# Recurrent merge tiles of a hybrid decoder layer: four of eight as two pairs by seven products

## The chip, the cores and the metric

The kernel runs on one core of one Trainium2 chip. The metric is the device time of one execution in microseconds. Before the change it is 872.28 us, the median of 3 runs (871.96 to 872.85).

## The reference

One inference step of one decoder layer over 512 prompt positions and 8 samples, so 520 columns; all in float32. The parts that the change touches:

```python
z = rmsnorm(x, g1) @ w_in                  # 1024 x 6656, column blocks for three mixers and three gates
h, h_last = rg_lru(conv(b_x), ...)         # recurrent branch
yb = gelu(b_gate) * h                      # b_gate: 1024 columns of z
ga, gb, gc = split(sigmoid(gates))         # 3 x 1024 columns of z
merged = ga * (ya @ w_pa) + gb * (yb @ w_pb) + gc * (yc @ w_pc)
x = x + merged @ w_o
h = gelu(causal_dwconv(xn2 @ wg)) * (xn2 @ wu)      # FFN, 3072 columns
x = x + h @ wd
```

## The kernel before

Everything lies feature by column: a tile of an activation is 128 features by 520 columns, and a weight tile is 1024 x 128, that is eight blocks of 128 x 128 (`Chunk`). A float32 product is made of three matmuls in fp32r: high part by high part, high by low, low by high. The high part is a copy on ScalarE (`high`, L117), the low part the difference to it on VectorE (`low`, L126). A plain tile is 8 blocks x 3 x 2 halves of 260 columns, 48 matmuls.

**Pairs by seven products.** Two output tiles can be made together (`Pair`): weights and input are each cut into 2 x 2 quarters, and seven products of 12 matmuls replace the eight of a plain computation, 84 matmuls where two plain tiles take 96. The products need sums of weight quarters (`sums`, two arrays h2 and h3, on VectorE, and their high and low parts, L189 and L192) and seven forms of the input (`X`), four of which (numbers 2, 3, 4, 6) are sums and differences, each with a high and a low part (`operand`). The results are put together from three PSUM banks and copies of what bank 0 and bank 2 held on the way (`run_pair`, the copies at L267). Input 0, 1 and 5 are halves of tiles that are there anyway. Before the change the four pairs of recurrent gates (`T_GB`) and the FFN tiles from the fifth on are made this way.

**Order.** Time is counted in tiles: `now` goes on by 1 for a plain tile, 0.125 for each of its eight blocks, and by 0.25 for each product of a pair. Each step of a weight tile or a pair has a time ahead of its start (`steps`, in quarters; `at`), and each step behind an output a time after it (`after`). Steps are put into the engines' queues in order of these times, and each queue is worked off in order. A pair goes through `SEQ_PAIR`, its products and, between them, the quarters of one more plain tile (the "filler", or two half-length tiles in the FFN); the first two FFN pairs, whose low parts are made by DMA (`by_dma`), go through `SEQ_FIRST`.

**The stretch that is changed.** Four plain tiles of the recurrent gate (`bg_parts`, times 44 to 48), each followed by `bg_post`: gelu on ScalarE, multiplication with h on VectorE (L843), high part on ScalarE (L433), low part on VectorE (L434). Then four gate pairs of 2.75 tiles each, with the other four `bg_parts` as fillers; their outputs (`gb_out`) go through a sigmoid and to DRAM (`gbd`). Their sums of the input are made from rows that `rows_in` (L884) reads back from DRAM (`xsd`), at times 42 and 43 (`XG`), a step every 0.6. Then eight plain merge tiles (`w_pb`, times 59 to 67), each with `pb_post`: multiplication with the gate (L880), addition of the other branches (L881), high and low part. `pb_load` brings the gate and the sum of the other branches two tiles ahead, and at the fifth tile `reload_x` reads all eight tiles of x at once for the output projection. Then eight `w_o` tiles, the second norm, and the FFN. Its first tiles are plain; the first pair comes behind them, and its fillers take the inputs hh[0] to hh[3], which `u2_post` and `later_hilo` (L1044) make from the last plain tiles.

The tiles of activations share 57 buffers of one size.

## Time and profile before

| | |
|---|---|
| median of 3 runs | 872.28 us |
| profiled execution, its own time | 872.23 us |
| its span | 870.5 us |
| mean granted TensorE clock | 0.993 |
| TensorE busy | 853.9 us, 7072 matmuls |
| VectorE busy | 620.3 us, 953 instructions |
| ScalarE busy | 476.9 us, 728 instructions |
| GpSimd busy | 159.2 us, 241 instructions |
| DMA | 124.89 MB, mean 143 GB/s |

The span is from the first to the last instruction of the profiled execution. The profile also divides it into stretches, lists what ended each engine's idle time (its releaser), and gives instructions in order of time. A matmul's end is modelled, so consecutive matmuls overlap in the list; what counts is the distance of their starts.

### The profile page before, as it was taken

The page shows a single profiled execution, that of the slowest core. Times are in us where ns is not written, and L with a number is a line of the kernel's source. Part 1 is how long each engine was busy: PE and PEld are TensorE (multiplying, and loading weights), DVE is VectorE, ACT ScalarE, POOL GpSimd, SP SyncE. Part 2 cuts the span into 40 slices and gives each one's busy share as a digit, 9 for nine tenths or more (in the row PEclk, how much of TensorE's full clock was granted, in tenths as well). Part 3 has the DMA queues.
Part 4 walks back from the last instruction along what each step waited for, and adds up shares of the span by engine and source line. Part 5 has one row for each costly group of instructions (what it writes and reads, how often), then busy time and mean ns, then how long its engine had stood idle before and what let it go on. Part 6 is the DMA issues. An engine that isn't in the chain of part 4 may idle for free.

```text
span 870.5 us, 17032 instructions
## 1 busy us (share of the span) xinstructions
PE 853.9 (98%) x7072; PEld 847.8 (97%) x7072; DVE 620.3 (71%) x953; ACT 476.9 (55%) x728; POOL 159.2 (18%) x241
## 2 busy tenths in 40 slices
PE   8999999999999999999999989999999999999996
PEld 7999999999999999999999989999999999999995
DVE  5797998698773876455553995776777777768655
ACT  7555464478341565542346785646656556556542
POOL 0522412111114000150012111011011110110143
PEclk9999999999999999999999999999999999999997
DMA  8464234322246633583349776555655555555642
GB/s 279 143 212 123 66 105 137 124 94 88 83 111 181 182 129 105 171 324 116 123 158 235 159 178 136 143 133 122 159 110 145 137 112 155 135 121 150 156 99 99
DMA packets 42254, 124.89 MB, mean 143 GB/s; under 512 B 5289, under 2 KB 8873, under 8 KB 42153
## 3 DMA queue, kind: packets, MB, share of 16 engines
q1 hardware_dynamic: 25872, 83.08, 30.6%
q0 software_dynamic: 14784, 39.17, 20.4%
q10 hardware_dynamic: 1520, 1.57, 0.5%
q8 instruction: 55, 0.90, 0.4%
q14 instruction: 23, 0.18, 0.1%
HBM read 100.09 MB, written 24.09 MB: 143 GB/s over the span
## 4 chain that ended last, share of the span: by engine, by line
PE 85%; DVE 8%; ACT 4%; issue 1%; DMA 1%; SPq 0%; POOL 0%; DVEq 0%; ACTq 0%; POOLq 0%
PE pj L211 57%; PE pa L263 15%; PE c L263 7%; PE pf L263 4%; PE lru L211 1%; DVE wl L192 1%; DVE b L993 1%; ACT wh L189 1%; DVE d L827 1%; DVE fc L971 1%; DVE bg L843 1%; DMA x<-in_x 1%; ACT yb_h L433 0%; ACT wh L117 0%; ACT L842 0%
## 5 line engine op out<-in xcount | busy, mean ns | idle before, releaser
L126 DVE TENSOR_TENSOR wl<-raw,wh 128x1024 fp32r<-128x1024 f32 (+1 forms) x96 | 111.7, 1168 | 10.4 <-ACT wh L117 9.9
L211 PE MATMUL pj<-xn_h,wh 128*128 128x260 f32 x576 | 116.5, 284 | 0.1
L211 PE MATMUL pj<-xn_h,wl 128*128 128x260 f32 x576 | 115.9, 282 | 0.6 <-DVE wl L126 0.6
L211 PE MATMUL pj<-xn_l,wh 128*128 128x260 f32 x576 | 116.1, 283 | 0.0
L117 ACT ACTIVATE wh<-raw 128x1024 fp32r<-128x1024 f32 (+1 forms) x106 | 105.2, 1000 | 2.5 <-DMA raw<-in_w_in 2.5
L211 PEld LDWEIGHTS pj<-xn_h,wl 128*128 128x128 f32 x576 | 88.7, 188 | 0.8 <-DVE wl L126 0.8
L211 PEld LDWEIGHTS pj<-xn_l,wh 128*128 128x128 f32 x576 | 88.9, 189 | 0.0
L211 PEld LDWEIGHTS pj<-xn_h,wh 128*128 128x128 f32 x576 | 88.6, 188 | 0.3 <-ACT r L557 0.3
L1107 POOL DMA_DIRECT2D x1d<-dn x40 | 34.5, 862 | 274.2 <-ACT dn L1106 264.5
L211 PE MATMUL pj<-h_h,wh 128*128 128x260 f32 x384 | 82.8, 283 | 1.5 <-ACT h_h L1047 1.5
L211 PE MATMUL pj<-h_l,wh 128*128 128x260 f32 x384 | 83.0, 284 | 1.2 <-DVE h_l L1048 1.2
L211 PE MATMUL pj<-h_h,wl 128*128 128x260 f32 x384 | 82.6, 283 | 0.0
L211 PEld LDWEIGHTS pj<-h_h,wh 128*128 128x128 f32 x384 | 61.5, 188 | 1.9 <-ACT h_h L1047 1.9
L211 PEld LDWEIGHTS pj<-h_l,wh 128*128 128x128 f32 x384 | 61.5, 189 | 1.7 <-DVE h_l L1048 1.7
L211 PEld LDWEIGHTS pj<-h_h,wl 128*128 128x128 f32 x384 | 61.6, 189 | 0.0
L192 DVE TENSOR_TENSOR wl<-sum,wh 128x1024 fp32r<-128x1024 f32 x48 | 58.5, 1219 | 0.0
L189 ACT ACTIVATE wh<-sum 128x1024 fp32r<-128x1024 f32 x48 | 50.4, 1049 | 0.0
L166 DVE TENSOR_TENSOR wl<-raw,wh 128x1024 fp32r<-128x1024 f32 x22 | 26.9, 1225 | 30.7 <-ACT wh L160 30.7
L971 DVE SCALAR_TENSOR_TENSOR fc<-fg,par,fc 128x512 f32<-128x512 f32 x48 | 36.0, 749 | 3.5 <-ACT fc L967 2.6
L704 ACT ACTIVATE gt<-pj 128x520 f32<-128x520 f32 x16 | 9.7, 605 | 52.3 <-PE pj L211 52.3
L267 ACT ACTIVATE m<-pa 128x260 f32<-128x260 f32 x48 | 18.3, 382 | 30.0 <-PE pa L263 29.8
L267 ACT ACTIVATE k<-pa 128x260 f32<-128x260 f32 x24 | 9.3, 387 | 44.1 <-PE pa L263 44.1
(467 smaller groups left out, 2590.3 us busy)
## 6 DMA issues: line engine op xcount, KB each, us to landing
raw<-in_w_in SPq DMA_DIRECT2D x50, 512.0 KB, 3.7
raw<-in_wg SPq DMA_DIRECT2D x24, 512.0 KB, 4.0
raw<-in_wu SPq DMA_DIRECT2D x24, 512.0 KB, 4.0
raw<-in_wd SPq DMA_DIRECT2D x24, 512.0 KB, 5.3
x1d<-dn POOLq DMA_DIRECT2D x40, 260.0 KB, 4.9
mgd<-gt POOLq DMA_DIRECT2D x16, 260.0 KB, 4.9
raw<-in_w_pb SPq DMA_DIRECT2D x8, 512.0 KB, 4.2
raw<-in_w_o SPq DMA_DIRECT2D x8, 512.0 KB, 3.6
```

The lines of the kernel that those rows point to most:

```text
L117: s.activation(self.h[:, q], self.raw[:, q], AF.Copy)
L126: v.tensor_sub(self.l[:, q], self.raw[:, q], f(self.h[:, q]))
L166: v.tensor_sub(self.new("h1", "wl"), self.raw[1], f(self.W["h1", "wh"]))
L189: s.activation(self.new(n, "wh"), self.s[n], AF.Copy)
L192: v.tensor_sub(self.new(n, "wl"), self.s[n], f(self.W[n, "wh"]))
L211: te.matmul(ps[:, h, :TH], ww, xx[h] if isinstance(xx, list) else xx[:, h * TH:(h + 1) * TH], start=first and n == 0, stop=last and n == 2)
L263: te.matmul(bank[b], ww, xx, start=seen[b] + j + e == 0, stop=i >= (6, 1, 5)[b] and j == 3 and e == 2, skip_group_check=True)
L267: s.activation(kept["AFC"[b] + str(seen[b])], bank[b], AF.Copy)
L704: s.activation(two(y), acc(ps), AF.Sigmoid)
L827: fn(o_[i], a[i], b[i])
L971: v.scalar_tensor_tensor(y[:, :SEQ], ext[:, r:r + SEQ], pc("fcw", r * MF + m), y[:, :SEQ], op0=ALU.mult, op1=ALU.add)
L1107: nc.gpsimd.dma_start(x1d[:, j, :], y, accum_op=ALU.add)
```

## The change

The eight merge tiles become two plain ones (0, 1), a pair (2, 3) with tile 4 as its filler and a pair (5, 6) with tile 7. Their inputs are yb: halves of it as they are, and sums and differences made from rows that are read back from DRAM. For that each yb is stored there (`ybd`) when it is made. `rows_in` and `sum_operands` now serve both inputs; for yb they come at 58.4 and 59.375, a step every 0.25, with the second and third combination exchanged. `pb_out` puts together a merge pair's outputs: `pb_post`'s work in halves.

One more plain gate tile comes ahead of the gate pairs (five, to 49), so that the gate pairs begin at 49, 51.75, 54.5 and 57.25; the fourth has no filler and takes 1.75. The merge tiles begin at 59 and 60, the merge pairs at 61 and 63.75, `w_o` at 66.5. The gates' own operands move from 42 and 43 to 41.5 and 42.5.

In `bg_post` the gelu, the multiplication, the high part and the low part of tiles 5 to 7 come a quarter apart. A filler's high and low part come a quarter earlier in all pairs but the first two of the FFN. x is read a tile at a time, two tiles ahead of its `w_o` tile. `SEQ_FIRST` begins with products 0 and 1 and has the fillers behind them, and `later_hilo` treats all tiles alike.

The diff, cut to its core:

```diff
@@ run_pair, run_jobs
-        out = gb_out(out) if isinstance(out, int) else out
+        out = out()
         for x in SEQ_FIRST if pair.by_dma else SEQ_PAIR:
             if isinstance(x, int):
                 product(x)
+            elif fill:
+                filler(*x)
             else:
-                filler(*x)
+                continue
             now[0] += 0.25
...
-                for dt, fn in zip((-4.25, -3.5, -3.25) if c.by_dma else (-2.25, -0.75, -0.5), (c.load, c.high, c.low)):
+                for dt, fn in () if c is None else zip((-4.25, -3.5, -3.25) if c.by_dma else (-2.25, -1, -0.75), (c.load, c.high, c.low)):
                     at(t1 + dt, fn)
-                t1 += 2.75
+                t1 += 2.75 if fill else 1.75
@@ bg_post
+        h, l = yb[j] = A(f"yb{j}_h", F32R), A(f"yb{j}_l", F32R)
+        e = 0.25 if j > 4 else 0
         s.activation(two(y), acc(ps), AF.Gelu_apprx_tanh)
-        v.tensor_mul(y, y, hs[j])
-        yb[j] = hilo(y, f"yb{j}_")
+        def times():
+            v.tensor_mul(y, y, hs[j])
+            nc.gpsimd.dma_start(ybd[:, j, :], y)
+        after(e, times)
+        after(2 * e, lambda: s.activation(h, y, AF.Copy))
+        after(3 * e, lambda: v.tensor_sub(l, y, f(h)))
@@ new
+    def pb_out(m):
+        tmp = [A("c") for _ in range(2)]
+        def split(i):
+            ma, y = pbs.pop(m + i)
+            h, l = mg[m + i] = A(f"mg{m + i}_h", F32R), A(f"mg{m + i}_l", F32R)
+            v.tensor_add(y, y, ma)
+            s.activation(h, y, AF.Copy)
+            after(0.25, lambda: v.tensor_sub(l, y, f(h)))
+        def out(n, a, b):
+            i, h = int(n[1]) - 1, int(n[2]) - 1
+            c = slice(h * TH, h * TH + TH)
+            y, o_ = pbs[m + i][1], tmp[i][:, c]
+            if n == "c11":
+                v.scalar_tensor_tensor(y[:, c], a, -1.0, y[:, c], op0=ALU.mult, op1=ALU.mult)
+                after(0.25, lambda: split(0))
+                return
+            add_parts(n, o_, a, b)
+            if n == "c12":
+                after(0.25, lambda: v.tensor_mul(y[:, c], o_, y[:, c]))
+            if n == "c22":
+                def rest():
+                    v.tensor_mul(y, y, tmp[1])
+                    after(0.25, lambda: split(1))
+                after(0.25, rest)
+        return out
@@ rows_in(src), sum_operands(step), was gate_operands
+        if step < 0.5:
+            steps[2:6] = steps[4:6] + steps[2:4]
+        in_turn(steps, [step] * len(steps))
+    for e, src in ((XG, xsd), (XB, ybd)):
+        at(e[0], lambda src=src: rows_in(src))
+        at(e[1], lambda e=e: sum_operands(e[2]))
...
-    for j in range(4):
+    for j in range(5):
         job([bg_parts(j)], lambda ps, j=j: bg_post(j, ps))
     for i in range(4):
         m = T_GB + 2 * i
-        pair_job(Pair(t["w_in"][m], t["w_in"][m + 1]), XB, 2 * i, [(bg_parts(4 + i), lambda ps, j=4 + i: bg_post(j, ps))])
-    for j in range(8):
-        def pre(j=j):
-            pb_load(j + 2)
-            if j == XLOAD:
-                reload_x()
-        job([(Chunk(t["w_pb"][j], KD, timed=True), 0, lambda k: yb[k])], lambda ps, j=j: pb_post(j, ps), pre)
+        pair_job(Pair(t["w_in"][m], t["w_in"][m + 1]), seven(xn), lambda i=i: gb_out(2 * i),
+                 [(bg_parts(5 + i), lambda ps, j=5 + i: bg_post(j, ps))] if i < 3 else [])
+    for j in range(2):
+        job([pb_parts(j)], lambda ps, j=j: pb_post(j, ps), lambda j=j: pb_load(j + 2))
+    def pb_pair(m):
+        pb_load(m + 2)
+        if m == 2:
+            after(1, lambda: pb_load(5))
+            after(1.5, lambda: pb_load(6))
+        else:
+            for j in range(2):
+                after(1.5 + j / 2, lambda j=j: x_load(j))
+        return pb_out(m)
+    for m in (2, 5):
+        pair_job(Pair(t["w_pb"][m], t["w_pb"][m + 1]), seven(yb), lambda m=m: pb_pair(m),
+                 [(pb_parts(m + 2), lambda ps, j=m + 2: pb_post(j, ps))])
@@ later_hilo
-        t0 = 0 if m == MP - 1 else 0.25
-        after(t0, lambda: s.activation(h, y, AF.Copy))
-        after(t0 + 0.25, lambda: v.tensor_sub(l, y, f(h)))
+        after(0.25, lambda: s.activation(h, y, AF.Copy))
+        after(0.5, lambda: v.tensor_sub(l, y, f(h)))
@@ constants
-SEQ_FIRST = ((0, 0), 0, (0, 1), 3, (1, 0), 2, (1, 1), 1, 4, 5, 6)
+SEQ_FIRST = (0, 1, (0, 0), 3, (0, 1), 2, (1, 0), 4, 5, 6, (1, 1))
 SEQ_PAIR = (0, (0, 0), 3, 2, (0, 1), 1, 4, 5, (1, 0), 6, (1, 1))
-XG = (42, 43, 0.6)
+XG, XB = (41.5, 42.5, 0.6), (58.4, 59.375, 0.25)
```

`w_o` tiles get `x_load(j + 2)` as their first step in place of `reload_x`.

## Rows read from the trace of the kernel before

**Rows 1.** The page, busy time of TensorE's matmuls: us, share of the span, instructions.

```profile
PE 853.9 (98%) x7072; PEld 847.8 (97%) x7072; DVE 620.3 (71%) x953; ACT 476.9 (55%) x728; POOL 159.2 (18%) x241
```

**Rows 2.** The chain that ended last, in order of time: start, length, what. This piece covers most of the merge tiles and `w_o`.

```profile
372.41 97.81 PE pj L211 x816
```

**Rows 3.** What TensorE waited for over the whole span: us in total, times, longest.

```profile
PE pa L263 <- DVE wl L192: 2.4, 4, 0.7
...
PE pj L211 <- ACT h_h L1047: 1.5, 2, 0.9
...
PE pj L211 <- DVE h_l L1048: 1.2, 1, 1.2
```

**Rows 4.** TensorE in order of time: two waits in the first gate pair; then the second gate pair, from its first matmul (323.19) to its fourth block, product 2. Columns: start, us, instruction, and in brackets the idle time before it and its releaser.

```profile
308.67 0.51 PE L211 MATMUL pj<-xn_h,wl 128*128 128x260 f32 x2 [0.55 <-DVE wl L126]
...
311.83 0.39 PE L263 MATMUL pa<-X20h,wl 128*128 128x260 f32 x1 [0.24 <-DVE wl L192]
...
323.19 0.29 PE L263 MATMUL pa<-xn_h,wh 128*128 128x260 f32 x1
...
327.66 0.28 PE L263 MATMUL pa<-X20l,wh 128*128 128x260 f32 x1
328.66 0.39 PE L263 MATMUL pa<-X20h,wl 128*128 128x260 f32 x1 [0.72 <-DVE wl L192]
```

**Rows 5.** TensorE in order of time in the first FFN pair: product 0 (514.48), the second half of the first filler, the end of product 3 and the filler behind it (524.01).

```profile
514.48 0.28 PE L263 MATMUL pa<-X00h,wh 128*128 128x260 f32 x1
...
516.60 0.50 PE L211 MATMUL pj<-h_h,wh 128*128 128x260 f32 x2 [0.54 <-ACT h_h L1047]
518.29 0.51 PE L211 MATMUL pj<-h_l,wh 128*128 128x260 f32 x2 [1.18 <-DVE h_l L1048]
...
519.97 0.67 PE L211 MATMUL pj<-h_h,wh 128*128 128x260 f32 x2 [0.94 <-ACT h_h L1047]
...
524.01 0.40 PE L211 MATMUL pj<-h_h,wh 128*128 128x260 f32 x2
```

**Rows 6.** Busy time by stretch, 521 to 522 us: length, then busy us and instructions of TensorE, its weight loads, VectorE, ScalarE and GpSimd, then the granted TensorE clock (1.00 is 2.4 GHz), the DMA share and GB/s.

```profile
521.00:522.00 1.00, 1.00 (x6) 1.00 (x6) 0.96 (x3) 0.68 (x3) 0.84 (x1) 0.50 0.87 160
```

**Rows 7.** VectorE in order of time around the start of the second gate pair.

```profile
320.90 1.22 DVE L126 TENSOR_TENSOR wl<-raw,wh 128x1024 fp32r<-128x1024 f32 x1
325.36 0.70 DVE L843 TENSOR_TENSOR bg<-bg,h 128x520 f32<-128x520 f32 x1 [3.25 <-ACT bg L842]
326.76 0.70 DVE L434 TENSOR_TENSOR yb_l<-bg,yb_h 128x520 fp32r<-128x520 f32 x1 [0.70 <-ACT yb_h L433]
327.38 1.22 DVE L192 TENSOR_TENSOR wl<-sum,wh 128x1024 fp32r<-128x1024 f32 x1
```

**Rows 8.** ScalarE there.

```profile
323.43 1.28 ACT L842 ACT_TABLE_LOAD   x1
324.72 0.60 ACT L842 ACTIVATE bg<-pj 128x520 f32<-128x520 f32 x1
```

**Rows 9.** ScalarE in the first FFN pair, in order of time, and VectorE's low part of the same input.

```profile
518.35 1.04 ACT L160 ACTIVATE wh<-raw 128x1024 fp32r<-128x1024 f32 x1
519.30 0.62 ACT L1047 ACTIVATE h_h<-fc 128x520 fp32r<-128x520 f32 x1
519.83 1.04 ACT L98 ACTIVATE wl<-wh 128x1024 fp32r<-128x1024 f32 x1
...
519.95 0.70 DVE L1048 TENSOR_TENSOR h_l<-fc,h_h 128x520 fp32r<-128x520 f32 x1
```

**Rows 10.** VectorE in order of time, instructions without idle time between them: operands and low parts ahead of the first gate pair, weight sums ahead of the third. The distance of starts is what one costs in a full queue.

```profile
303.82 0.69 DVE L803 SCALAR_TENSOR_TENSOR X20l<-d,X20h 128x520 fp32r<-128x520 f32 x1
...
305.04 1.30 DVE L827 TENSOR_TENSOR d<-d,b 128x520 f32<-128x520 f32 x2
306.26 1.22 DVE L192 TENSOR_TENSOR wl<-sum,wh 128x1024 fp32r<-128x1024 f32 x1
307.40 1.22 DVE L126 TENSOR_TENSOR wl<-raw,wh 128x1024 fp32r<-128x1024 f32 x1
...
328.52 0.69 DVE L181 TENSOR_TENSOR sum<-raw 128x512 f32<-128x512 f32 x1
329.24 0.69 DVE L182 TENSOR_TENSOR sum<-sum,raw 128x512 f32<-128x512 f32 x1
329.85 0.68 DVE L184 TENSOR_TENSOR sum<-raw 128x512 f32<-128x512 f32 x1
```

**Rows 11.** VectorE in order of time, the output of one plain merge tile.

```profile
385.36 0.70 DVE L880 TENSOR_TENSOR gb<-pj,gb 128x520 f32<-128x520 f32 x1 [1.42 <-PE pj L211]
386.09 0.70 DVE L881 TENSOR_TENSOR gb<-gb,ga 128x520 f32<-128x520 f32 x1
387.50 0.70 DVE L434 TENSOR_TENSOR mg_l<-gb,mg_h 128x520 fp32r<-128x520 f32 x1 [0.71 <-ACT mg_h L433]
```

**Rows 12.** GpSimd in order of time: the eight row loads for the gates' operands, and a gate load that waits. Then DMA issues by line with the median us from issue to landing: the row loads (270 to 290 us) and the gate stores (355 to 400 us).

```profile
273.24 6.03 POOL L889 DMA_DIRECT2D b<-xsd  x8
...
361.22 0.54 POOL L876 DMA_DIRECT2D gb<-gbd  x1 [1.73 <-DMA gbd<-gt]
...
b<-xsd POOLq DMA_DIRECT2D x8, 260.0 KB, 6.7
...
gbd<-gt POOLq DMA_DIRECT2D x4, 260.0 KB, 4.5
```

More of the change, by code (lines that the diff above doesn't have):

```diff
@@ L305, in run_jobs @@
                     at(t1 + dt / 4, fn)
-                c = pairs[n][3][0][0][0]
-                for dt, fn in zip((-4.25, -3.5, -3.25) if c.by_dma else (-2.25, -0.75, -0.5), (c.load, c.high, c.low)):
+                fill = pairs[n][3]
+                c = fill[0][0][0] if fill else None
+                for dt, fn in () if c is None else zip((-4.25, -3.5, -3.25) if c.by_dma else (-2.25, -1, -0.75), (c.load, c.high, c.low)):
                     at(t1 + dt, fn)
-                t1 += 2.75
+                t1 += 2.75 if fill else 1.75
                 if n == mx_end - 1:
@@ L506, in rstd_bcast @@
         return out
-    mgd, gbd, xsd, x1d = (dp.tile([P, KD, T], F32, name=n) for n in ("mgd", "gbd", "xsd", "x1d"))
+    mgd, gbd, xsd, ybd, x1d = (dp.tile([P, KD, T], F32, name=n) for n in ("mgd", "gbd", "xsd", "ybd", "x1d"))
     xg, xn, rs1 = [], [], []
@@ L868, in out @@
                 for j in range(2):
-                    after(0.25 + j / 4, lambda j=j: pb_load(j))
+                    after(0.5 + j / 4, lambda j=j: pb_load(j))
         return out
     def pb_load(j):
-        if j < 8:
-            pbs[j] = A(f"ga{j}"), A(f"gb{j}")
-            for d, src in zip(pbs[j], (mgd, gbd)):
-                nc.gpsimd.dma_start(d, src[:, j, :])
+        pbs[j] = A(f"ga{j}"), A(f"gb{j}")
+        for d, src in zip(pbs[j], (mgd, gbd)):
+            nc.gpsimd.dma_start(d, src[:, j, :])
     def pb_post(j, ps):
@@ L882, in pb_post, with rows_in @@
         mg[j] = hilo(y, f"mg{j}_")
-    def rows_in():
+    def pb_out(m):
[23 more added lines that the diff above has]
+        return out
+    xs = {}
+    def rows_in(src):
         xs["b"] = {(i, h): [A(f"b{i}{h}_{n}") for n in range(2)] for i in range(2) for h in range(2)}
@@ L888, in rows_in, with sum_operands @@
                 k = 4 * i + 2 * n
-                nc.gpsimd.dma_start(two(q[n]), xsd[:, k:k + 2, h * TH:h * TH + TH])
-    xs = {}
-    def gate_operands():
+                nc.gpsimd.dma_start(two(q[n]), src[:, k:k + 2, h * TH:h * TH + TH])
+    def sum_operands(step):
         b = xs.pop("b")
@@ L899, in gate_operands, with half, seven, pb_parts @@
                  lambda: onto(v.tensor_sub, d, d, b21), lambda: operand(6, d)]
-        in_turn(steps, [XG[2]] * len(steps))
-    at(XG[0], rows_in)
-    at(XG[1], gate_operands)
-    def xn_half(i, h):
-        return lambda k: [q[:, h * TH:h * TH + TH] for q in xn[4 * i + k]]
-    XB = [xn_half(0, 0), xn_half(1, 0), op_of(2), op_of(3), op_of(4), xn_half(1, 1), op_of(6)]
+        if step < 0.5:
[4 more added lines that the diff above has]
+        at(e[1], lambda e=e: sum_operands(e[2]))
+    def half(q, i, h):
+        return lambda k: [x[:, h * TH:h * TH + TH] for x in q[4 * i + k]]
+    def seven(q):
+        return [half(q, 0, 0), half(q, 1, 0), op_of(2), op_of(3), op_of(4), half(q, 1, 1), op_of(6)]
     def bg_parts(j):
         return Chunk(t["w_in"][T_BG + j], KD, timed=True), 0, lambda k: xn[k]
-    for j in range(4):
+    def pb_parts(j):
+        return Chunk(t["w_pb"][j], KD, timed=True), 0, lambda k: yb[k]
+    for j in range(5):
         job([bg_parts(j)], lambda ps, j=j: bg_post(j, ps))
@@ L928, in trunk_kernel, with x_load @@
     st2 = [None]
-    def reload_x():
-        for j in range(8):
+    def x_load(j):
+        if j < 8:
             x1[j] = A(f"xr{j}")
@@ L944, in trunk_kernel @@
     for j in range(8):
-        job([(Chunk(t["w_o"][j], KD, timed=True), 0, lambda k: mg[k])], lambda ps, j=j: wo_post(j, ps))
+        job([(Chunk(t["w_o"][j], KD, timed=True), 0, lambda k: mg[k])], lambda ps, j=j: wo_post(j, ps), lambda j=j: x_load(j + 2))
     rs2 = [None]
@@ L1179, in mixer @@
         if m >= MP:
-            pair_job(Pair(src[m], src[m + 1], m == MP), XP, out(m),
+            pair_job(Pair(src[m], src[m + 1], m == MP), XP, lambda: out(m),
                      [(wd_parts(p, j), lambda ps, j=j: dn_post(p, j, ps, (0, 1))) for j in js])
@@ L1235 @@
 XSTEP = (0.125, 0.375)
-XLOAD = 4
-XG = (42, 43, 0.6)
+XG, XB = (41.5, 42.5, 0.6), (58.4, 59.375, 0.25)
 LRU0, LRUS, GLEAD, CLEAD = 8, 3.25, 6, 4
```

## The prediction

> **What bounds the kernel now.** I read the page's busy times first: TensorE is busy for 853.9 of 870.5 us [rows 1], so the kernel is as long as its matmul stream plus the holes in it. The profiled execution took 872.23 us (span 870.5 and 1.7 us around it), 0.05 us under the median of 872.28, so a sum made against the profile can be set beside the median as it stands. The rate comes from the chain of work: 816 matmuls in 97.81 us, 0.12 us each, 1.44 us for a block of 12 [rows 2]. The list of TensorE's waits then gives the holes that matter here [rows 3], and its timeline their places. In each gate pair it waits for the low part of the h3 weights (L192). A matmul is drawn 0.28 us long but the next starts after 0.12, so each idle figure is 0.16 short of what is lost: 0.72 is a loss of 0.88, and the first pair's 0.55 and 0.24 are 0.71 and 0.40 [rows 4]. Together 1.1 + 3 x 0.88 = 3.76 us. The other hole is the first FFN pair: from 514.48 to 524.01 there are 36 matmuls, 4.32 us of work in 9.53, so 5.2 us are lost [rows 5], 3.8 in waits and about 1.4 because the granted clock stood at 0.50, 1.2 GHz, behind them [rows 6].
>
> Why do the gate pairs wait? VectorE's queue runs in order. The filler's weights are done at 322.1; then it stands 3.25 us before the multiply of bg, which waits for a gelu, 0.70 more before yb_l, and only at 327.38 comes the low part that TensorE wants at 327.78 [rows 4, 7]. The gelu itself starts at 324.72, behind a table load [rows 8].
>
> **Removed work.** Two pairs of seven products take 2 x 84 matmuls where four tiles took 4 x 48: 24 fewer, 2.88 us of pure stream. All other matmuls stay.
>
> **Gate pairs.** With the steps a block apart VectorE's order is multiply, h3's low part, yb_l. In the second pair the low part then starts at 326.0 and ends at 327.1, before 327.78: the 0.88 goes, there and in the third. The first pair comes a tile later and its operands half a tile earlier, which takes 2.4 us of operand work (two low parts, one difference of 1.22) out of VectorE's queue ahead of it; I put both its losses (1.1) at nothing. The fourth pair has no tile between: it wants h3 two blocks after its start, not three, and the multiply is still ahead. Put its start at 0. Ahead of its gelu ScalarE has one weight high part less (no tile between) and one more (the first merge tile's), so the times of the second pair hold: there the multiply ends 2.8 after the pair's start at 323.19, and the low part would end at 4.0 [rows 4, 7, 8]. It is wanted at 3.1. So 0.9 is lost there as before. Its copies out of PSUM have one block (1.44) to hide a copy of 0.4; that is enough. Gain: 1.1 + 2 x 0.88 = 2.9; bounds 1.1 (only the first) and 3.8 (all).
>
> **First FFN pair.** Two products now come first, the tiles between later. On the times of before, product 0 starts a block ahead of 514.48, at 513.05; the second half of the first tile between at 518.83, and its last input, hh[3], is wanted at 519.55. VectorE and ScalarE are no faster: the multiply of that input is still among the work that ends with h_l at 519.95 [rows 9]. On ScalarE its high part stood between L160 and L98, from 519.30; set a quarter later it comes behind the copy of product 0 (0.3) and L98 (0.95), starts at 520.55 and ends at 521.05, and h_l ends at 521.7. Lost: 1.55 + 0.4 = 1.95 in place of 5.2, a gain of 3.25 if the clock stays up; 1.85 if it falls again.
>
> **The new operands, and who pays.** The products need sums and differences of yb. Each yb goes to DRAM and comes back in rows, as xsd does now. That adds 8 stores and 8 loads of 260 KB on POOL's queue (some 0.75 us each to issue [rows 12]), 4 combinations and 8 high and low parts; and each weight pair adds 4 sums and its own low parts. All of that sits between the end of the fourth gate pair and the first merge pair, where two plain tiles give 11.5 us of cover.
>
> I walk VectorE's queue there. The fourth pair's product 5 ends at 9.5 (six blocks and the 0.9), its two outputs at 10.3; nothing queued behind can start sooner. Then, in the order of their due times, up to the end of the second plain tile: weight sums 2.53 (0.72 and three of 0.6 [rows 10]); low parts of weights, three of 1.13 and one of 0.6, 4.0 [rows 10]; low parts of operands 3 x 1.22 and combinations 4 x 1.22, 8.5 [rows 10]; the output of the first plain tile, 2.8 (two steps of 0.73, 0.68 standing for ScalarE, 0.62 [rows 11]). That is 17.9 us. Behind it stand the output of the second plain tile, 2.8, and h3's low part, 1.13: 10.3 + 21.8 = 32.1. TensorE begins the merge pair at 22.5 and wants that low part at 27.1 (three blocks and two matmuls later). **It waits 5.0 us.** Product 0's copy, behind the second tile's high part on ScalarE, is done at about 30.7 and hides in this. No operation of the sum is new in kind. Bounds: 3.6 if both stands for ScalarE are filled; with waits for rows (below) up to 8.
>
> After a wait of that size I expect the clock to fall as it did at 520 [rows 6] and charge 1.4 us for it (bounds 0 and 1.4). The Trainium skill ("TensorE: Matmul & The Clock Gate", "Part 1: The HAM clock gate") says that the throttled state is the default, released by activity and taken back by idleness; by it this change pays wherever it turns a short wait into a long one. The rows bear that out at 520 and not at the gate pairs' 0.88.
>
> The second merge pair waits too. From the end of the first one's product 5, VectorE has two outputs 0.8, two low parts 2.27, two multiplies 1.0, an add 0.62, c11 0.4, a low part 0.62, an add 0.62, the output of the tile between 2.0 (no more than its own chain), a low part 0.62 and h3 1.13, with 0.6 of ScalarE between: about 10.6. TensorE wants it six blocks and 0.24 later, 8.9. It waits 1.7; bounds 0 and 2.5. The first W_o tile wants its sixth input 8.2 us after the second pair's product 5, and that ends there by the same count at 8.2 to 8.3: nothing.
>
> **Small edits.** Reading x by tile leaves two tiles (11.5 us) between issue and use; the row loads nearest to it land in 6.7 us [rows 12]. Cost nothing; without that cover a late x would hold wo_post, not TensorE. The filler's high and low parts a quarter earlier change no order of TensorE's waits: nothing. One table switch less on ScalarE, off the path: nothing.
>
> **The sum.** -2.9 (matmuls) -2.9 (gate pairs) -3.25 (FFN pair) +5.0 +1.4 (first merge pair and clock) +1.7 (second) = -0.95. 872.23 - 0.95 = **871.3 us**.
>
> **Rivals.**
> *Rows late (slower).* The last yb is stored when its multiply is done, 2.9; the store lands about 4.5 us later, the next loads on POOL stand behind it, as gb stood 1.73 us for a gbd store [rows 12]. Then three more rows are issued, and the last lands 6.7 later, at 16.5; VectorE wants it at 16.9. The loads of the merge pair's weights, the gates and the products so far share the same DMA engines just then, and the tiles that the rows go into may still be held by a gate store. From 16.9 on each us late is a us of the merge pair's wait. 4 us late: **875.3**. For it: the 0.4 of slack; against: b needed 6.7 in a stretch just as full. Chance 0.20.
>
> *The clock falls three times.* If the waits of 1.7 and 1.95 us bring it down as well, 2 x 1.4 is added: **874.1**. The rows have 2.7 us of idle in 4 us ahead of the fall and none behind the 0.88 [rows 4 to 6]; these two lie between. Chance 0.10. The rule of the Trainium skill cited above (same page, same section) points this way.
>
> *The wait is shorter and the clock stays.* VectorE fills the stands; 3.6 and no fall: **868.5**. Chance 0.18.
>
> *No wait at the merge pairs.* If VectorE has the sums done ahead, only gains are left: 872.23 - 9.05 = **863.2**. Against it: c22 and c12 of the fourth gate pair stand ahead of them in the queue. Chance 0.07.
>
> *The change does not do what it says.* The multiply still holds h3 back in the second and third gate pair (slack 0.7): +1.8, **873.1**. Chance 0.05.
>
> **How the numbers follow.** The forecast has 0.40; its own range, from the bounds of its terms, is 869 to 874. About 0.2% (1.74 us) is what a measurement of this kernel can tell from no change: faster is under 870.5, slower over 874.0. Faster: 0.18 + 0.07 + a third of the forecast, 0.38. Slower: most of the late rows, half of the three falls, a little of the forecast, 0.24. Within: 0.38. The range 867.5 to 875.8 leaves out the case without waits and the later half of the late rows.
>
> **What would show it.** In the list of TensorE's waits L192's 2.4 us fall to one of about 0.7 in the gate pairs and a new one of 4 to 5 us at the third product of the first merge pair, VectorE busy without a hole for 20 us ahead of it, granted clock 0.50 for some 3 us behind it; another of 1.7 in the second pair; h_h and h_l of L1047 and L1048 down to about 1.5 and 0.4. VectorE idle for the b rows there would be the late rows. No L192 wait in the merge pairs would make the walk of the queue wrong; an unchanged one in the second gate pair, the reordering.

## The result, and the profile after

The changed kernel takes 878.47 us (median of 4 runs, 876.23 to 879.0) where the kernel before takes 872.35 on the same chip: a ratio of 1.0065, with a 95% interval of 1.0049 to 1.008. It is slower, and outside the predicted range of 867.5 to 875.8. The execution that was profiled took 876.23 us with a span of 874.5. The other three took 878.3 to 879.0; experiment 1 shows what sets them apart.

The first line of the page after, busy time by engine, to set beside [rows 1]:

```profile
PE 852.5 (97%) x7048; PEld 846.4 (97%) x7048; DVE 639.7 (73%) x989; ACT 485.5 (56%) x747; POOL 170.5 (19%) x257
```

TensorE has the 24 matmuls less, and yet the span is 4.0 us longer, so the holes have grown. The list of what TensorE waited for (us in total, times, longest) tells which, beside [rows 3]:

```profile
PE pa L263 <- ACT m L267: 4.8, 2, 4.3
PE pa L263 <- DVE wl L192: 3.5, 4, 1.7
```

TensorE in order of time, the waiting matmuls alone. They lie in the first gate pair, the fourth, the first merge pair (two), the second (two), at the first `w_o` tile, and in the first FFN pair (two):

```profile
314.12 0.51 PE L211 MATMUL pj<-xn_h,wl 128*128 128x260 f32 x2 [0.41 <-DVE wl L126]
...
317.27 0.39 PE L263 MATMUL pa<-X20h,wl 128*128 128x260 f32 x1 [0.24 <-DVE wl L192]
...
364.46 0.39 PE L263 MATMUL pa<-X20h,wl 128*128 128x260 f32 x1 [0.75 <-DVE wl L192]
...
391.83 0.58 PE L263 MATMUL pa<-X20h,wh 128*128 128x260 f32 x1 [4.32 <-ACT m L267]
...
393.43 0.59 PE L263 MATMUL pa<-X20h,wl 128*128 128x260 f32 x1 [0.79 <-DVE wl L192]
...
411.99 0.39 PE L263 MATMUL pa<-X20h,wh 128*128 128x260 f32 x1 [0.45 <-ACT m L267]
414.19 0.39 PE L263 MATMUL pa<-X20h,wl 128*128 128x260 f32 x1 [1.70 <-DVE wl L192]
...
430.42 0.51 PE L211 MATMUL pj<-mg_l,wh 128*128 128x260 f32 x2 [0.87 <-DVE mg_l L902]
...
528.03 0.50 PE L211 MATMUL pj<-h_h,wh 128*128 128x260 f32 x2 [1.41 <-ACT h_h L1102]
528.76 0.51 PE L211 MATMUL pj<-h_l,wh 128*128 128x260 f32 x2 [0.23 <-DVE h_l L1103]
```

The releaser named at 391.83 is ScalarE's copy of product 0 out of PSUM, but it is one of two that are late; VectorE's low part of h3 comes behind it at 393.43. VectorE's queue ahead of them, in part:

```profile
370.31 0.43 DVE L836 TENSOR_TENSOR gt<-c,m 128x260 f32<-128x260 f32 x1 [1.35 <-PE c L263]
...
381.11 0.70 DVE L437 TENSOR_TENSOR mg_l<-gb,mg_h 128x520 fp32r<-128x520 f32 x1 [0.76 <-ACT mg_h L436]
382.06 1.22 DVE L192 TENSOR_TENSOR wl<-sum,wh 128x1024 fp32r<-128x1024 f32 x1 [0.25 <-ACT wh L189]
...
388.19 1.30 DVE L830 TENSOR_TENSOR d<-d,b 128x520 f32<-128x520 f32 x2
389.41 0.69 DVE L890 TENSOR_TENSOR gb<-pj,gb 128x520 f32<-128x520 f32 x1
...
391.53 0.70 DVE L437 TENSOR_TENSOR mg_l<-gb,mg_h 128x520 fp32r<-128x520 f32 x1 [0.70 <-ACT mg_h L436]
392.15 1.22 DVE L192 TENSOR_TENSOR wl<-sum,wh 128x1024 fp32r<-128x1024 f32 x1
```

From 370.3 to 393.3 VectorE stands for 1.7 us in all, in three stands, each for a high part from ScalarE, none for a row from DRAM. The second plain tile's matmuls end where the pair begins, at 383.05; the first step of its output, L890, comes at 389.41 because operand work is queued ahead of it. ScalarE waits for that output in its own in-order queue, and the copy of product 0 stands behind its high part:

```profile
390.87 0.64 ACT L436 ACTIVATE mg_h<-gb 128x520 fp32r<-128x520 f32 x1 [3.33 <-DVE gb L891]
391.41 0.37 ACT L267 ACTIVATE m<-pa 128x260 f32<-128x260 f32 x1
```

Busy time by stretch (columns as in [rows 6]), behind the first wait and at two later places (behind the second merge pair's wait and the FFN pair's):

```profile
392.00:393.00 1.00, 0.63 (x2) 0.33 (x2) 1.00 (x2) 1.00 (x3) 0.00 (x0) 0.50 0.00 0
416.00:417.00 1.00, 1.00 (x11) 1.00 (x10) 0.00 (x0) 0.08 (x1) 0.00 (x0) 1.00 0.79 131
532.00:533.00 1.00, 1.00 (x11) 1.00 (x10) 0.65 (x1) 0.32 (x1) 0.00 (x0) 1.00 1.07 190
```

The granted clock is down after the first merge pair's wait (0.50; matmuls start 0.22 us apart there and 0.12 elsewhere) and, in this execution, up at the other two places.

**Losses by place.** For each stretch below: the time between the first and the last start of a matmul in it, less 0.1204 us for each matmul, a little over the 0.1199 of [rows 2], which on the longest stretch makes 0.2 us. That holds the waits, the 0.16 which a wait costs beside its idle figure, and the time lost to a low clock. A figure within 0.4 of zero is the error of the method. All are of the profiled executions; the times and ratios are of all runs, each ratio against runs of the kernel before made beside them (medians 872.35 to 872.98).

| kernel | median us | ratio, 95% interval | gates 1 to 3 | gate 4 | merge 1 | merge 2, `w_o` | FFN 1 |
|---|---|---|---|---|---|---|---|
| before | 872.35 | | 3.3 | 0.9 | -0.2 | -0.2 | 4.9 |
| after | 878.47 | 1.0065 (1.0049 to 1.008) | 1.0 | 1.0 | 8.2 | 3.6 | 2.0 |
| after_again | 877.97 | 1.0059 (1.0042 to 1.0075) | 1.1 | 0.9 | 7.8 | 5.2 | 3.5 |
| rows_free | 878.93 | 1.0074 (1.0059 to 1.0089) | 1.1 | 1.0 | 7.5 | 5.2 | 3.7 |
| plain_merge | 867.34 | 0.9941 (0.9927 to 0.9956) | 1.1 | 0.9 | -0.2 | 0.0 | 2.0 |
| no_operands | 870.63 | 0.9974 (0.9961 to 0.9988) | 1.1 | 1.0 | 0.2 | 3.6 | 2.1 |
| ffn_order | 869.47 | 0.9964 (0.995 to 0.9978) | 2.9 | 0.9 | -0.3 | -0.4 | 2.1 |
| gelu_apart | 869.35 | 0.996 (0.9945 to 0.9975) | 0.7 | -0.1 | -0.1 | -0.2 | 5.3 |
| late_ops | 874.88 | 1.0028 (1.0016 to 1.004) | 1.0 | 1.0 | 2.0 | 8.6 | 2.2 |
| post_late | 874.11 | 1.0018 (1.0009 to 1.0028) | 1.0 | 1.0 | 7.5 | 1.1 | 3.6 |
| best_plain | 864.24 | 0.9905 (0.989 to 0.9919) | 0.1 | 0.1 | 0.1 | -0.1 | 0.7 |
| best_pairs | 872.31 | 0.9997 (0.9982 to 1.0012) | -0.1 | 1.0 | 5.2 | 4.7 | 0.8 |
| best_pairs_h3 | 872.19 | 0.9996 (0.9986 to 1.0005) | -0.2 | -0.1 | 7.1 | 2.7 | 1.5 |
| pairs_dve | 867.58 | 0.9947 (0.993 to 0.9963) | -0.1 | 1.0 | 3.5 | 1.6 | 0.6 |

### The profile page after: what moved, and what is told of

Its sections match the earlier page's. It is cut to its first block, busy times and chain, and to the rows that moved or that the text cites. A ratio compares the mean times of both kernels' runs of the same rounds, so it can differ in the third digit from the quotient of the medians.

```text
span 874.5 us, 17079 instructions
## 1 busy us (share of the span) xinstructions
PE 852.5 (97%) x7048; PEld 846.4 (97%) x7048; DVE 639.7 (73%) x989; ACT 485.5 (56%) x747; POOL 170.5 (19%) x257
## 3 DMA queue, kind: packets, MB, share of 16 engines
q10 hardware_dynamic: 1520, 1.57, 0.5%
## 4 chain that ended last, share of the span: by engine, by line
PE 85%; DVE 8%; ACT 3%; issue 2%; DMA 1%; POOL 0%; SPq 0%; DVEq 0%; ACTq 0%; POOLq 0%
PE pj L211 54%; PE pa L263 16%; PE c L263 8%; PE pf L263 4%; PE lru L211 1%; DMA ga<-mgd 1%; DVE b L1049 1%; DVE wl L192 1%; DVE d L830 1%; DVE fc L1027 1%; DVE wl L126 1%; DMA x<-in_x 0%; PE vm L766 0%; ACT wh L189 0%; PE po L211 0%
## 5 line engine op out<-in xcount | busy, mean ns | idle before, releaser
L126 DVE TENSOR_TENSOR wl<-raw,wh 128x1024 fp32r<-128x1024 f32 (+1 forms) x92 | 106.7, 1166 | 6.7 <-ACT wh L117 6.2
L117 ACT ACTIVATE wh<-raw 128x1024 fp32r<-128x1024 f32 (+1 forms) x102 | 101.1, 998 | 2.3 <-DMA raw<-in_w_in 2.3
L192 DVE TENSOR_TENSOR wl<-sum,wh 128x1024 fp32r<-128x1024 f32 x52 | 63.4, 1219 | 2.3 <-ACT wh L189 2.3
L189 ACT ACTIVATE wh<-sum 128x1024 fp32r<-128x1024 f32 x52 | 54.5, 1049 | 0.0
L166 DVE TENSOR_TENSOR wl<-raw,wh 128x1024 fp32r<-128x1024 f32 x24 | 29.4, 1225 | 33.5 <-ACT wh L160 33.4
```

The lines of the kernel that those rows point to most:

```text
L117: s.activation(self.h[:, q], self.raw[:, q], AF.Copy)
L126: v.tensor_sub(self.l[:, q], self.raw[:, q], f(self.h[:, q]))
L166: v.tensor_sub(self.new("h1", "wl"), self.raw[1], f(self.W["h1", "wh"]))
L189: s.activation(self.new(n, "wh"), self.s[n], AF.Copy)
L192: v.tensor_sub(self.new(n, "wl"), self.s[n], f(self.W[n, "wh"]))
```

## The experiments

**1. The same kernel again, and rows that wait for nothing.** The theory was the queue of VectorE: what is in it ahead of h3's low part makes the wait. Two rivals would also make a long wait there: a wait that varies from run to run, which would account for the 876.23 and the 879, and rows that come late from DRAM. after_again is the changed kernel unedited; in rows_free the rows for the merge pairs are read from `xsd`, which was written long before, so their loads stand behind no store (the sums are then of other data).

```diff
-    for e, src in ((XG, xsd), (XB, ybd)):
+    for e, src in ((XG, xsd), (XB, xsd)):
```

> The changed kernel once more, for a second profile. In the first one TensorE lost 8.1 us at the first merge pair (5.8 in waits, 2.3 at half clock behind them), 2.5 at the second and 1.0 at the first W_o tile, and that execution took 876.23, while the median is 878.47. Theory: the 2.2 us between them are further falls of the clock, behind the second pair's wait or the FFN pair's; then a profile of an execution near 878.5 shows the same waits within 0.3 us and one or two more stretches at 0.50. Rival: the waits themselves are longer in the slower executions (DMA landings that vary); then the list of waits differs by 2 us and the clock does not.

> The rows are read from the normed x in DRAM, which has long been there, instead of yb (so the merge pairs' results are others): no load waits for a store. Same work on every engine and the same bytes. Rows late: the wait at the first merge pair falls by 2 us or more, 870 to 874. VectorE's queue: unchanged, 876 to 879.

after_again: TensorE in order of time at three of the waits, and the three stretches:

```profile
391.88 0.59 PE L263 MATMUL pa<-X20h,wh 128*128 128x260 f32 x1 [4.32 <-ACT m L267]
...
413.91 0.39 PE L263 MATMUL pa<-X20h,wl 128*128 128x260 f32 x1 [1.70 <-DVE wl L192]
...
529.28 0.51 PE L211 MATMUL pj<-h_h,wh 128*128 128x260 f32 x2 [1.38 <-ACT h_h L1102]
```

```profile
392.00:393.00 1.00, 0.69 (x2) 0.38 (x2) 1.00 (x2) 1.00 (x3) 0.00 (x0) 0.50 0.00 0
416.00:417.00 1.00, 1.00 (x7) 1.00 (x6) 0.00 (x0) 0.07 (x1) 0.00 (x0) 0.50 0.94 213
532.00:533.00 1.00, 1.00 (x6) 1.00 (x6) 0.49 (x1) 0.00 (x0) 0.67 (x2) 0.50 0.75 147
```

The waits are those of after, to 0.1 us; the clock is not. It is down in three stretches where after had it down in one, and that makes the span 877.4 where it was 874.5: two more falls of about 1.5 us each in the table. The waits don't vary, then; whether a wait of 1.4 to 2.2 us is followed by a fall of the clock does. The mean granted clock of each execution of after and after_again says the same: 0.991 and 0.992 in the three at 876.2 to 876.9 us, 0.987 to 0.989 in the five at 878.3 to 879.1. rows_free has the same waits again (4.33, 0.79, 0.45, 1.70, 0.87) and three falls, and is no faster. Late rows are out.

**2. The pairs back to plain tiles, and the pairs without their operand work.** plain_merge takes the two pairs, their rows and their stores out and leaves the rest of the change in. no_operands keeps the pairs, rows and weights and leaves out the sums and differences of yb and their high and low parts (halves of yb stand in for them).

```diff
 plain_merge
-            nc.gpsimd.dma_start(ybd[:, j, :], y)
...
-    for e, src in ((XG, xsd), (XB, ybd)):
+    for e, src in ((XG, xsd),):
...
-    for m in (2, 5):
-        pair_job(Pair(t["w_pb"][m], t["w_pb"][m + 1]), seven(yb), ...)
+    for j in range(2, 8):
+        job([pb_parts(j)], lambda ps, j=j: pb_post(j, ps), lambda j=j: pre(j))
 no_operands
-        at(e[1], lambda e=e: sum_operands(e[2]))
+        if src is xsd:
+            at(e[1], lambda e=e: sum_operands(e[2]))
     def seven(q):
+        if q is yb:
+            return [half(q, 0, 0), half(q, 1, 0), half(q, 0, 1), half(q, 0, 0), half(q, 0, 1), half(q, 1, 1), half(q, 1, 0)]
```

> The change with its eight merge tiles plain: no pairs there, no stores and rows of yb; the gate pairs, the apart steps, x by tile and the FFN order stay. If the merge pairs alone lose (first, second, W_o tile), the rest shows its own gain: 1.8 in the second and third gate pair and 3.2 in the FFN pair, 872.3 - 5.0 = 867.3. If the other parts cost something that the waits do not show, 870 or more.

> The sums and differences of yb and their high and low parts are left out (halves of yb stand in for them, so the merge pairs' results are others); stores, row loads, matmuls and weight work stay. Theory (VectorE's queue is too long): 8.5 us less of it ahead of h3's low part ends it at 24.4 after the fourth gate pair's start where 27.1 is wanted; no wait and no clock fall at the first merge pair, while the second pair's 2.5 and W_o's 1.0 stay: 868 to 870. Rival (rows late, DMA traffic): nothing changes, 876 to 879. Second rival (the copy out of PSUM behind the second tile's high part is enough): a wait of over 2 us stays at the third product.

Without the pairs the change is worth 0.6%: 867.34, as expected. So the pairs, with 24 matmuls less, cost 11.1 us against plain tiles. Without the operand work the list has no wait in the first merge pair, and 8.2 us of loss become 0.2; the second pair and `w_o` keep theirs. The copy of product 0 is in time there too, so ScalarE's order alone did not make the wait. TensorE in order of time, no_operands:

```profile
403.76 0.39 PE L263 MATMUL pa<-yb_h,wh 128*128 128x260 f32 x1 [0.37 <-ACT m L267]
405.97 0.39 PE L263 MATMUL pa<-yb_h,wl 128*128 128x260 f32 x1 [1.70 <-DVE wl L192]
...
422.19 0.50 PE L211 MATMUL pj<-mg_l,wh 128*128 128x260 f32 x2 [0.87 <-DVE mg_l L902]
```

Two causes, then: VectorE's operand work for the first pair, and something else for the second. The ten runs of no_operands spread from 867.33 to 873.73, with a median of 870.63 where 868 to 870 was expected; the profiled one is the fastest, with the clock at 1.00 behind the second pair's wait, so its row in the table is that of the best case.

**3. Which of the queue's steps are in the way.** late_ops puts the last two combinations of yb, and the operand between them, behind h3's low part (the products that need them are products 4 and 6, later in the pair). post_late gives the output of the tile inside a merge pair half a tile's delay, so that the pair's own outputs, h3 and the copy of product 0 go ahead of it.

```diff
 late_ops
-            steps[2:6] = steps[4:6] + steps[2:4]
-        in_turn(steps, [step] * len(steps))
+            steps[2:6] = steps[4:6] + [lambda: None] + steps[2:4]
+        in_turn(steps, [step] * 4 + [0.875 if step < 0.5 else step] + [step] * 4)
 post_late
-                 [(pb_parts(m + 2), lambda ps, j=m + 2: pb_post(j, ps))])
+                 [(pb_parts(m + 2), lambda ps, j=m + 2: after(0.5, lambda: pb_post(j, ps)))])
```

> The changed kernel, but the last two combinations of yb and operand 4 come behind the low part of the first merge pair's h3 instead of ahead of it: 3.7 us less in front of it, the same work in all. Theory (length of VectorE's queue up to that low part): the loss of 5.8 us at the third product falls to 2.2, and operand 4 and 6 are still in time: 878.4 - 3.6 = 874.8, and down to 872.5 where the clock no longer falls there. Rival (ScalarE or PSUM limits the pair): unchanged, 878.

> The changed kernel, but the output of a merge pair's filler comes half a tile later, behind the next pair's low part of h3 and behind the first pair tile's own low part. Theory: 2.7 us less in front of both; the second merge pair's 2.5 and the first W_o tile's 1.0 go, and with them the clock's fall behind the second pair: 878.4 - 3.5 - 1.5 = 873.4, the first merge pair as before. Rival (the second pair is late because the first one was): unchanged waits there, 878.

TensorE in order of time, late_ops, the two pairs; then post_late, the second pair and `w_o`:

```profile
388.22 0.39 PE L263 MATMUL pa<-X20h,wh 128*128 128x260 f32 x1 [0.47 <-ACT m L267]
389.81 0.39 PE L263 MATMUL pa<-X20h,wl 128*128 128x260 f32 x1 [1.08 <-DVE wl L192]
...
408.11 0.39 PE L263 MATMUL pa<-X20h,wh 128*128 128x260 f32 x1 [2.26 <-ACT m L267]
410.31 0.58 PE L263 MATMUL pa<-X20h,wl 128*128 128x260 f32 x1 [1.69 <-DVE wl L192]
```

```profile
412.27 0.39 PE L263 MATMUL pa<-X20h,wl 128*128 128x260 f32 x1 [0.45 <-DVE wl L192]
...
429.35 0.51 PE L211 MATMUL pj<-mg_l,wh 128*128 128x260 f32 x2 [0.22 <-DVE mg_l L437]
```

late_ops took the first pair's loss from 8.2 to 2.0, and the second pair's with `w_o` rose from 3.6 to 8.6, with the clock down there: the first pair starts its second half earlier, and the work that VectorE still has to do meets the second pair. What was moved was mostly a debt: 6.2 us less in the one place, 5.0 more in the next. The median, 874.88, is the 874.8 of the expectation, but not by its road: that had 3.6 us of gain at the first pair and nothing lost at the second. The agreement is luck. post_late shows the second cause by itself: with the output of the tile between out of the way, 2.2 us of idle become 0.45, and the first `w_o` tile's 0.87 becomes 0.22. It left the first pair alone.

**4. The two other parts alone, on the kernel before.** ffn_order has the new order of the first FFN pair and the later high and low part; gelu_apart has the steps of `bg_post` a quarter of a tile apart from tile 4 on.

```diff
 ffn_order
-SEQ_FIRST = ((0, 0), 0, (0, 1), 3, (1, 0), 2, (1, 1), 1, 4, 5, 6)
+SEQ_FIRST = (0, 1, (0, 0), 3, (0, 1), 2, (1, 0), 4, 5, 6, (1, 1))
-        t0 = 0 if m == MP - 1 else 0.25
+        t0 = 0.25
 gelu_apart
-        v.tensor_mul(y, y, hs[j])
-        yb[j] = hilo(y, f"yb{j}_")
+        h, l = yb[j] = A(f"yb{j}_h", F32R), A(f"yb{j}_l", F32R)
+        e = 0.25 if j > 3 else 0
+        after(e, lambda: v.tensor_mul(y, y, hs[j]))
+        after(2 * e, lambda: s.activation(h, y, AF.Copy))
+        after(3 * e, lambda: v.tensor_sub(l, y, f(h)))
```

> The kernel before with one part of the change: the first two FFN pairs begin with products 0 and 1, and the last input's high part comes a quarter later. Theory: the pair's loss falls from 5.2 to 2.0, 872.4 - 3.2 = 869.2, and up to 870.7 in executions in which the clock still falls behind the 1.4 us wait. Rival (the gain comes from the earlier start of everything in front): nothing below 871.5.

> The kernel before with another part alone: the gelu, the multiplication, the high and the low part of the four fillers' outputs a quarter apart. Theory (h3's low part stood behind yb_l in VectorE's queue): the 0.88 of the second, third and fourth gate pair go, the first pair's 1.1 stays, 872.4 - 2.6 = 869.8. Rival (the gelu's own lateness decides): 872 to 872.5.

Each is worth 0.4% by itself. ffn_order touches the FFN pair alone (4.9 to 2.1 in the table), gelu_apart the gate pairs alone (4.2 to 0.6 in the table; by the starts at the waits 3.76 to 0.85, that is 2.9 us, beside the 3.0 by which the profiled spans differ). There the fourth gate pair's wait goes too; that kernel still has a tile between the third pair and the fourth.

**5. What can be had.** best_plain is the kernel before with the steps apart from tile 2 on and the new `SEQ_FIRST`, its `t0` as before: no merge pairs. best_pairs keeps the pairs and has late_ops, post_late, `t0` as before, the steps apart from tile 2 on, and the four weight sums of the first merge pair on GpSimd. best_pairs_h3 is best_pairs with h3's low part half a tile earlier in every pair. pairs_dve is best_pairs with the sums back on VectorE.

```diff
 best_plain (with SEQ_FIRST as in ffn_order)
+        e = 0.25 if j > 1 else 0
 best_pairs (with late_ops and post_late)
-        e = 0.25 if j > 4 else 0
+        e = 0.25 if j > 1 else 0
-        pair_job(Pair(t["w_pb"][m], t["w_pb"][m + 1]), seven(yb), ...
+        pair_job(Pair(t["w_pb"][m], t["w_pb"][m + 1], eng=g if m == 2 else None), seven(yb), ...
 pairs_dve (best_pairs otherwise)
-                self.eng.tensor_add(...)    (four times)
+                v.tensor_add(...)
 best_pairs_h3
-(1, lambda: self.low("h3"))
+(-1, lambda: self.low("h3"))
```

> The kernel before with the parts that gained and no merge pairs: gelu steps a quarter apart for tiles 2 to 7, the new FFN order, and the last FFN input's high part at once as before. If each wait was one engine's queue order, the gate pairs' 3.8 go and the FFN pair's 5.2 fall to about 1: 872.5 - 8 = 864.5. If the gains hide one another: above 866.5.

> The changed kernel with the merge pairs kept and VectorE's queue made shorter: late operands 4 and 6, late filler outputs, the first merge pair's four weight sums on GpSimd (2.5 us less on VectorE), gelu steps apart for tiles 2 to 7, the last FFN input's high part at once. Theory (length of that queue): no more than 0.3 lost at the first merge pair, under 1 at the second, no fall of the clock; 872.5 - 2.9 - 2.9 - 4.2 + 1.3 = 863.8. Rival (GpSimd's own waits hold the sums back): a wait for L192 or L189 at the first merge pair, 868 or more.

> The kernel of best_pairs with the low part of h3 half a tile earlier in all pairs, ahead of what follows the previous pair. Theory: the fourth gate pair's 0.9 goes, and the merge pairs no longer wait for L192: 0.9 to 1.9 below best_pairs. Rival: something else now stands behind it and is late (the copy out of PSUM or the outputs of the pair before): no change or slower.

> The kernel best_pairs with the four weight sums of the first merge pair back on VectorE. It tells apart whether the adds on GpSimd cost VectorE more than they took from it. If they did: VectorE has 2.5 us of sums more and its other instructions at their usual length (L166 1.22 us, L175 0.68, a combination 0.65) in 372 to 381 us of the span; the waits of the first merge pair go from 3.0 us in three to about 1.6 in two (as in late_ops, 0.47 and 1.08), the second keeps about 2, the fourth gate pair 0.75 and the FFN pair 0.23: about 866 us without a fall of the clock, up to 868.5 with one. If the sums on GpSimd were a help after all (rival: the slow instructions belong to something else in that stretch), the first merge pair waits 2.5 us longer than in best_pairs, with clock falls as there: 873 to 876 us.

best_plain came as expected and beats both kernels by the widest margin: 864.24 us, ratio 0.9905. Of all the waits listed above one is left:

```profile
516.36 0.51 PE L211 MATMUL pj<-h_l,wh 128*128 128x260 f32 x2 [0.22 <-DVE h_l L1051]
```

best_pairs missed: 872.31 where 863.8 was expected. The rival had a time of 868 or more, but sums that are late for L189 or L192 as its cause; in the profile TensorE waits at the first merge pair for the weights of the tile between (1.62 us for ScalarE's L117, 0.71 for VectorE's L126), and 0.67 for L192. VectorE in order of time, best_pairs, in the stretch of the first merge pair's operands; then GpSimd there:

```profile
372.48 2.12 DVE L166 TENSOR_TENSOR wl<-raw,wh 128x1024 fp32r<-128x1024 f32 x1 [0.57 <-ACT wh L160]
374.52 1.78 DVE L175 TENSOR_TENSOR wlq<-raw,whq 128x512 fp32r<-128x512 f32 x1
...
377.44 4.16 DVE L830 TENSOR_TENSOR d<-d,b 128x520 f32<-128x520 f32 x2
```

```profile
373.58 2.16 POOL L182 TENSOR_TENSOR sum<-sum,raw 128x512 f32<-128x512 f32 x1
...
377.88 1.30 POOL L184 TENSOR_TENSOR sum<-raw 128x512 f32<-128x512 f32 x1
379.13 1.29 POOL L186 TENSOR_TENSOR sum<-sum,raw 128x512 f32<-128x512 f32 x1
```

pairs_dve has the sums back on VectorE, with nothing else changed. The same three lines in it:

```profile
373.55 1.22 DVE L166 TENSOR_TENSOR wl<-raw,wh 128x1024 fp32r<-128x1024 f32 x1
374.69 0.68 DVE L175 TENSOR_TENSOR wlq<-raw,whq 128x512 fp32r<-128x512 f32 x1
...
376.51 1.30 DVE L830 TENSOR_TENSOR d<-d,b 128x520 f32<-128x520 f32 x2
```

They take 3.2 us here and 8.1 in best_pairs: the 2.5 us of sums that left VectorE cost it 4.9. pairs_dve takes 867.58, 4.7 us under best_pairs, as its theory had it (866 without a fall of the clock, up to 868.5 with one; its profile shows one, at 390 to 393). best_pairs_h3 removed the fourth gate pair's loss (1.0 to -0.1), as meant, and gave it back in the first merge pair (5.2 to 7.1): no change in all, the rival's outcome. The first wait of that pair, in best_pairs and then in best_pairs_h3:

```profile
385.61 0.50 PE L211 MATMUL pj<-yb_h,wh 128*128 128x260 f32 x2 [1.62 <-ACT wh L117]
```

```profile
386.49 0.80 PE L211 MATMUL pj<-yb_h,wh 128*128 128x260 f32 x2 [3.85 <-ACT wh L117]
```

TensorE comes to that pair 1.4 us sooner (381.04 in place of 382.40), and the high part L117 that it needs comes 0.9 us later (it starts at 385.40 in place of 384.52): ahead of it in ScalarE's queue stands mg_h, which waits for VectorE's L891 (383.13 in place of 382.24). The low part that was moved stands behind this wait, at 389.02, and did not make it.

pairs_dve is still 3.3 us above best_plain. The table adds up: it loses 1.0, 3.5 and 1.6 us in the last gate pair and the merge pairs where best_plain loses next to nothing, 6.1 in all, and has 2.9 us of matmuls less.

## Why the prediction was wrong

The sum on record was -0.95; the profiled executions differ by 876.23 - 872.23 = +4.0. By term:

| term | predicted | measured | how |
|---|---|---|---|
| matmuls | -2.9 | -2.9 | 24 fewer |
| gate pairs | -2.9 | -1.9 | 3.76 lost before [rows 3, 4]; after 0.57 + 0.40 + 0.91 (idle and 0.16 each) |
| first FFN pair | -3.25 | -2.9 | table |
| first merge pair and clock | +6.4 | +8.2 | table |
| second merge pair | +1.7 | +2.5 | 0.45 and 1.70 of idle, 0.16 each |
| first `w_o` tile | 0 | +1.1 | 3.6 of the table less 2.5 |

The measured terms add up to +4.1. That execution had one fall of the clock in this stretch, as the forecast had; the median lies 2.2 us above it because most executions had more.

**The step that failed.** The mechanism was forecast, but the terms of the sum were too favourable: the first merge pair with its clock by 1.8 us, the first `w_o` tile by 1.1, the gate pairs by 1.0, the second merge pair by 0.8, the FFN pair by 0.35. All err to the same side and make 5.0 us. The 2.2 us above them are the further falls, which the forecast left to a rival.

**Right.** The steps apart freed the second and third gate pair, the fourth lost 0.9 as walked, and the FFN pair lost 1.57 + 0.39 in its two waits against 1.55 + 0.4. The place and the mechanism of the big loss were right: an in-order VectorE, full for 23 us (but for the 1.7 of stands) ahead of h3's low part, which ends the loss. The walk from the end of product 5 to the end of that low part gave 22.6 us; measured, 370.3 to 393.3, 23.0. No b row was waited for, against the first rival; rows_free shows it too.

**The wait list reads otherwise than forecast.** Expected was a wait of 4 to 5 us for L192 there. The list has 4.32 for the copy of product 0 and 0.79 for L192. The prediction had that copy done at about 30.7 behind the fourth gate pair's start and hidden in the other wait; it was done at 31.4, where TensorE was ready for product 2 at 26.9. An earlier low part of h3 alone would thus not have freed this place: the copy stands behind mg_h, and that behind the same VectorE queue.

**The first merge pair was mis-sized, by 1.8.** "9.5 (six blocks and the 0.9)" for the end of product 5 was 0.4 too early (370.31 is 9.9 behind the fourth pair's start, 360.42), and the walk was 0.4 too short, so the low part ended at 32.9, not 32.1. TensorE lost 5.6 in its two waits (by the starts, 387.23 to 391.83 and 392.21 to 393.43 less 0.12 each), in place of 5.0. The rest is the clock. It was charged 1.4, the loss behind the FFN pair of before [rows 6]. Here the clock stayed at 0.50 to 398.6, for 24 matmuls of 0.22 us, and 8.2 less 5.6 is 2.6. The bounds "0 and 1.4" took one instance for the ceiling.

**The second merge pair was mis-sized by 0.8, and `w_o` by 1.1.** Both walks give the output of the tile between 2.0 us ("no more than its own chain"). Its rows in after, at the second pair:

```profile
409.56 0.69 DVE L890 TENSOR_TENSOR gb<-pj,gb 128x520 f32<-128x520 f32 x1
...
411.69 0.70 DVE L437 TENSOR_TENSOR mg_l<-gb,mg_h 128x520 fp32r<-128x520 f32 x1 [0.70 <-ACT mg_h L436]
412.31 0.69 DVE L902 TENSOR_TENSOR mg_l<-gb,mg_h 128x520 fp32r<-128x520 f32 x1
```

It took 2.75, for VectorE stood 0.70 for its high part. post_late shows that this output held both: half a tile later, 2.2 us of idle are 0.45 and 0.87 is 0.22. For `w_o` the step that failed is "that ends there by the same count at 8.2 to 8.3: nothing": counted from the second pair's product 5 (421.53), the low part was done at 8.8 (430.29), and TensorE wanted it at 7.9 (429.39), not at 8.2. A walk that ends within 0.1 us of its limit is no zero.

**The first gate pair did not gain.** "I put both its losses (1.1) at nothing", since 2.4 us of operand work left VectorE's queue. In after the output of the fourth of the five plain tiles (L850 and L855, with a stand of 0.70 between) stands in that place, and 1.0 stays. VectorE in order of time, after:

```profile
309.69 0.69 DVE L850 TENSOR_TENSOR bg<-bg,h 128x520 f32<-128x520 f32 x1
311.09 0.70 DVE L855 TENSOR_TENSOR yb_l<-bg,yb_h 128x520 fp32r<-128x520 f32 x1 [0.70 <-ACT yb_h L854]
311.71 1.22 DVE L192 TENSOR_TENSOR wl<-sum,wh 128x1024 fp32r<-128x1024 f32 x1
312.85 1.22 DVE L126 TENSOR_TENSOR wl<-raw,wh 128x1024 fp32r<-128x1024 f32 x1
```

best_plain and pairs_dve, which put that tile's steps apart too, lose nothing there. The walk struck out what left the queue and did not put in what came there.

**The clock was given too little chance.** The rival of three falls had 0.10 and 874.1; in the profiled executions of after_again and rows_free it holds, and their times agree with most runs of after. With it and the measured terms the median follows: 876.2 and two falls of 1.0 to 1.5 us give 878.2 to 879.2. The same waits of 1.4 and 1.7 us were followed by 0.50 in after_again and by 1.00 in after. The gate pairs' 0.9 were followed by a fall in neither. The rule of the Trainium skill that the prediction cited ("TensorE: Matmul & The Clock Gate", "Part 1: The HAM clock gate"), that idleness takes the clock back, agrees with the rows at these two waits in after_again and not in after. What decides between the two outcomes at one and the same wait no run here shows.

## What to carry to other kernels

Look at the queue that already releases TensorE's waits before adding work to it. Here 24 matmuls saved (2.9 us) did not pay for 8.5 us of operand work on VectorE. Moving work later passed most of the debt to the next wait (late_ops). With late operands, late outputs and steps apart together (pairs_dve) the pairs came to 867.58, still behind the 864.24 of best_plain, which has none. Separate the parts before judging a change: two parts here gained 0.4% each and hid behind a third that lost 11 us. A wait of over a us on TensorE should carry a chance of a fall of the clock: at 1.4 to 2.2 us it came in some executions and not in others. And a walk that ends within a few tenths of its limit should carry a term, not a zero.

## What the runs showed that was not expected

**GpSimd's adds slow VectorE.** In best_pairs VectorE's two combinations take 4.16 us beside two adds on GpSimd, where they take 1.30 alone. The two of VectorE and the two of GpSimd (1.30 + 1.29) make 3.9 one after the other: they hardly overlapped. GpSimd's L182 took 2.16 beside L166, and 1.30 is what its like took. The Trainium skill ("SBUF — State Buffer", "Who interferes with whom") states that a VectorE instruction with two SBUF inputs contends with a GpSimd instruction that reads SBUF, and calls the ports that they share an exclusive lock. All of these are additions or subtractions of two tensors, and in best_pairs the durations agree. In best_pairs_h3 another instruction of VectorE meets the two adds (1.30 each), a low part that takes 0.69 elsewhere:

```profile
377.10 4.16 DVE L808 TENSOR_TENSOR X31l<-d,X31h 128x520 fp32r<-128x520 f32 x1
```

That is 0.87 more than the three lengths together, so taking turns accounts for most of the delay and not for all of it; the rest stays open.

**One wait, two outcomes.** Ten runs of no_operands, whose longest wait in the profiled run is 1.70 us, spread over 6.4 us (867.33 to 873.73), while four runs of best_plain, with 0.22 us of waits, lie within 0.3. The clock makes part of the spread: its mean is 0.996 in the fastest run and 0.991 in the slowest. But runs with a mean of 0.991 lie from 870.57 to 873.73, and the ten of best_pairs spread over 6.4 us too, with 0.993 at 868.92 and 0.991 at 875.36, where two further falls in the changed kernel (0.991 and 0.987) made 2.8 us. What makes the rest is not shown.
